# The running maximum of the cached pages, spread over the partitions by one rounded-type product of a high and a low part

## The chip, the cores and the metric

The kernel runs on one core of one Trainium2 chip. The metric is the device time of one execution in microseconds. The kernel must return the ten outputs of the reference; its inputs are float32.

## The reference

One inference step of one decoder layer. A prompt of 1024 tokens and eight sequences with eight new tokens each pass through an input projection; its columns feed a gated linear attention and a multi-head latent attention with eight heads. An output projection, a gated feed-forward part with a causal convolution, and a per-layer embedding follow.

The change concerns the latent attention of the eight sequences. Each has 64 cached pages of 128 positions, found by a page table. The softmax over the cached positions runs block by block, with a running maximum:

```python
def combine(a, b):
    m1, l1, acc1 = a
    m2, l2, acc2 = b
    m = jnp.maximum(m1, m2)
    c1 = jnp.exp(m1 - m)
    c2 = jnp.exp(m2 - m)
    return m, l1 * c1 + l2 * c2, acc1 * c1[..., None] + acc2 * c2[..., None]
...
def body(carry, phys):
    c = pool_ckv[phys]
    r = pool_krope[phys]
    k, v = latent_to_kv(c, r, w_kvup, g_kn)
    return combine(carry, block_stats(q, k, v, None)), None
```

In `block_stats`, m is the maximum of the block's scores, p the exponential of the scores less m, l their sum and acc the product of p with the values.

## The kernel before, in words

float32 products are made in most places by splitting both operands into a high part in the rounded type (`F32R`) and a low part, the remainder; `mm3` (lines 138 to 141) then sums three rounded products. `split` (line 114) makes the parts: a cast on ScalarE and a subtraction on VectorE or GpSimd.

The cached pages are worked through in 64 blocks, eight for each sequence; a block is eight pages and, in the first block of a sequence, the new tokens too. The generator `cache_stream` (line 678) runs its stages staggered over three blocks: `stage_load` fetches the pages by an indirect DMA; `pre` transposes the latents (`turn`, line 515) and makes the rope scores (`rope_scores`); `main` (line 543) makes the key products `ks`, squares them on ScalarE (line 560) and sums the squares on VectorE (line 565); `stage_b` (line 580) normalises the scores `sn`, a tile of 128 positions by pages by 64 pairs of head and token, and takes the maximum over the pages into `ml`, which holds the 64 columns twice (lines 598 and 599); `stage_c1` (line 606) handles the maximum; `stage_pv` multiplies by the latents.

In `stage_c1`, `ml` is transposed into PSUM (line 616), so that the 64 pairs lie on partitions, twice: 0 to 63 and 64 to 127. VectorE reduces over the positions and the earlier maximum `mo` into `m`, one column of 128 partitions (line 620 in the first block of a sequence, 622 in the others, there with an accumulator that is read by an instruction of its own). Line 625 spreads `m` over all partitions: the weights are the first 64 entries of `m`, repeated in 128 columns, and the moving operand is a 64x64 identity. The result, 128x64, is subtracted from the scores on VectorE (line 626); the exponential (628) and the split of the result (629, 630) follow. Line 635 works out the factor for the earlier sums from `m` and `mo`.

The blocks run beside the projections, the gated linear attention and the attention of the prompt (`dense`), which the loop at lines 1603 to 1614 interleaves with the blocks by a table of paces, and beside units of the output projection (`fill`) in the last blocks. The order on each engine's queue is set by the framework's planner, which simulates a timeline with its own costs of instructions. The feed-forward part comes behind all blocks.

`ones64`, four rows of 128 ones, is a source for a row of ones in the scratch tensor `dga`, written by three DMAs (lines 353 and, once for each half of the prompt, 857).

Of the kernel before, what the change touches and what calls it, by code (L numbers as in the profile page):

```python
# [8 lines left out]
F32 = mybir.dt.float32  # L9
F32R = mybir.dt.float32r  # L10
# [3 lines left out]
ALU = mybir.AluOpType  # L14
# [4 lines left out]
P = 128  # L19
D = 1024  # L20
T = 1024
# [3 lines left out]
R = NB * TS  # L25
# [19 lines left out]
def step_kernel(ctx: ExitStack, tc: tile.TileContext, A):  # L45
    nc = tc.nc
    pe, act, dve, pool, sp = nc.tensor, nc.scalar, nc.vector, nc.gpsimd, nc.sync
# [4 lines left out]
    def ctile(shape, dt, name):  # L52
        return const.tile(shape, dt, name=name, tag=name)
# [3 lines left out]
    ident = ctile([P, P], F32, "ident")  # L57
# [33 lines left out]
    dga = dram.tile([17, NTOK], F32, name="dga")  # L91
# [69 lines left out]
    def fold_rows(wk, ps, n, out, tag, bufs=None):  # L161
        t = wk.tile([R, 512], F32, tag=tag, name=tag, bufs=bufs)
        act.copy(t[:, :n], ps[R:2 * R, :n])
        dve.tensor_tensor(out, ps[0:R, :n], t[:, :n], ALU.add)
# [19 lines left out]
    cp = ph1.enter_context(tc.tile_pool(name="cp", bufs=1, side="right"))  # L184

    def pd(shape, name):
        return psD.tile(shape, F32, tag="d", name=name)
# [4 lines left out]
    def pm(shape, name):  # L192
        return psM.tile(shape, F32, tag="m", name=name)

    def cst(shape, dt, name):
        return cp.tile(shape, dt, name=name, tag=name)
# [4 lines left out]
    mv = [[cst([P, 576], F32R, f"mv{i}{s}") for s in "hl"] for i in range(2)]  # L201
    qbd = [[cst([P, 4, 64], F32R, f"qbd{i}{s}") for s in "hl"] for i in range(2)]
    chl = [cst([P, 9, 258], F32R, "chl")]
    ones64 = cst([4, P], F32, "ones64")
    pool.memset(ones64, 1.0)
    pool.memset(chl[0][:, :, 256:258].bitcast(F32), 1.0)
    newc = cst([P, 1, P], F32, "newc")
# [66 lines left out]
    def mm_lat(ps, x, w, first, last):  # L274

        if len(w.shape) == 3:
            ps = ps.rearrange("p (a c) -> p a c", a=2)
        pe.matmul(ps, x, w, start=first, stop=last)  # L278
# [64 lines left out]
    def sample_u(u, w):  # L343
        ps = pm([P, 512], "ps_sm")
        for k in range(8):
            for s in range(2):
                mm_lat(ps[:, :NL], xTs[:, k, :], w[s][k], k + s == 0, k + s == 8)
        fold_rows(wk, ps, NL, u[:R], "st", 3)
        pt = pm([P, 512], "pt_us")
        pe.transpose(pt[:16, :R], u[:R, 0:16], ident[:R, :R])  # L350
        act.copy(gaTs, pt[:16, :R])
        sp.dma_start(dga[1:17, T:], gaTs)
        sp.dma_start(dga[0:1, T:], ones64[0:1, 0:R])

    def sample_latents(u):
        cq = wk.tile([P, H, 96], F32, tag="qt", name="cq_s").rearrange("p h c -> p (h c)")[:, 0:256]
# [249 lines left out]
    def stage_c1(o):  # L606

        nt = o.nt
        sb = o.sn[:, :nt, :]
        mt = pm([P, 512], "mt")  # L610
        drain = o.n - NB * 8 + 3
        if drain == 1:
            fill(49 - z["units"])
        elif drain == 2:
            fill(2)
        pe.transpose(mt[:, 0:P], o.ml.rearrange("p a c -> p (a c)"), ident)
        m = cp.tile([P, 1], F32, tag="bm", name="bm", bufs=4)
        mo = state.get(o.b)
        if mo is None:
            dve.tensor_reduce(m, mt[:, 0:P], AX.X, ALU.max)  # L620
        else:
            dve.tensor_scalar(mt[:, 256:256 + P], mt[:, 0:P], mo, None, ALU.max, ALU.max, accum_out=m)
        if drain > 0:
            fill(1)
        pe.matmul(mt[:, P:P + 64], m[0:64].broadcast_to([64, P]), ident[0:64, 0:64], start=True, stop=True)
        dve.tensor_tensor(sb, sb, mt[:, P:P + 64].unsqueeze(1).broadcast_to([P, nt, 64]), ALU.subtract)
        phl = cp.tile([P, 9, P], F32R, tag="phl", name="phl", bufs=1)
        act.activation(sb, sb, AF.Exp)
        act.copy(phl[:, :nt, 0:64], sb)  # L629
        pool.tensor_tensor(phl[:, :nt, 64:128], sb, phl[:, :nt, 0:64].bitcast(F32), ALU.subtract)  # L630
        o.phl = phl
        o.t = None
        if mo is not None:
            o.t = cp.tile([P, 1], F32, tag="mb", name="mb", bufs=4)
            act.activation(o.t, m, AF.Exp, bias=mo, scale=-1.0)
        state[o.b] = m
# [41 lines left out]
    def cache_stream():  # L678
# [7 lines left out]
        for n in range(N + 2):  # L686
            z["block"] = n
            if n + 2 < N:
                blk[n + 2] = stage_load(*todo[n + 2], n + 2)
            if n < N:  # L690
                pre(blk, blk[n], 4)
                main(blk[n], 0)
            if 0 <= n - 2:
                stage_pv(blk[n - 2])
            if 0 <= n - 1 < N:
                stage_b(blk[n - 1])
            yield
            if n < N:
                if blk[n].nt == 9:
                    pre(blk, blk[n], 8)  # L700
                    main(blk[n], 4)
                    pre(blk, blk[n + 1], 0)
                    main(blk[n], 8)
                else:
                    if n + 1 < N:
                        pre(blk, blk[n + 1], 0)
                    main(blk[n], 4)
            if 0 <= n - 1 < N:
                stage_c1(blk[n - 1])
            if 0 <= n - 2:  # L710
                stage_c2(blk.pop(n - 2))
            yield
# [12 lines left out]
    def prompt_half(hf):  # L725
# [3 lines left out]
        hs = slice(hf * 512, hf * 512 + 512)  # L729
# [45 lines left out]
        if hf == 0:  # L775
            sample_x()
            load_x()
            wl = load_lat([chl[0][:, 2 * k:2 * k + 2, 0:NL // 2] for k in range(4)])
            load_x()
            load_constants()  # L780
            u = wk.tile([P, NL], F32, tag="u", name="u_s")
            sample_u(u, wl)
# [67 lines left out]
        def rank():  # L850
            pt = pd([P, 4, P], "pt_ga")
            for i in range(4):
                pe.transpose(pt[:16, i], lat[:, i, 0:16], ident)
            ga = wk.tile([P, 512], F32, tag="st", name="ga", bufs=3)
            act.copy(ga[:16], pt[:16].rearrange("p i c -> p (i c)"))
            sp.dma_start(dga[1:17, hs], ga[:16])
            sp.dma_start(dga[0, hs].rearrange("(a b) -> a b", a=4), ones64[0:4])

        def norm_latents(i):
            t = 4 * hf + i  # L860
# [87 lines left out]

        yield from mix(PLAN[0])
        rank()  # L950
        for i in range(4):
            norm_latents(i)
# [642 lines left out]
    def fill(n):  # L1595
        for _ in range(n):
            z["units"] += next(z["fill"], done) is None
# [302 lines left out]
    h, hs = z["h"], z["hs"]  # L1900
# [334 lines left out]
def build(arrays):  # L2235
    import concourse.bacc as _bacc

    nc = _bacc.Bacc("TRN2", target_bir_lowering=False, num_devices=1)
    A = {k: nc.dram_tensor(k, v.shape, mybir.dt.from_np(v.dtype), kind="ExternalInput").ap() for k, v in arrays.items()}
    for k, s in _OUTS:  # L2240
        A[k] = nc.dram_tensor(k, s, F32, kind="ExternalOutput").ap()
    with tile.TileContext(nc, schedule_with_timeline_sim=True) as tc:
        step_kernel(tc, A)
    return nc
# [11 lines left out]
```

## Time and profile before

| | us |
|---|---|
| median of 3 runs | 2219.15 (2218.44 to 2219.22) |
| profiled execution, device time | 2221.39 |
| its span, first to last instruction | 2219.6 |
| TensorE busy in the span | 2134.6 |
| VectorE busy in the span | 1666.6 |
| ScalarE busy in the span | 1369.1 |
| GpSimd busy in the span | 1227.5 |

The granted TensorE clock of the profiled execution was 0.984 of full speed. In profile lines PE is TensorE's products, PEld its weight loads, DVE VectorE, ACT ScalarE, POOL GpSimd, SP SyncE. A line in order of time has the start and the duration in us, engine, line of the kernel, operation, output tile and inputs, sizes and a count; in brackets stand the idle time before it and what ended that. A line of a group has the smallest, median and largest duration in ns and the starts of the first and the last. Products overlap in TensorE's pipeline, so the distance of their starts tells more than their durations.

### The profile page before, as it was taken

The page shows a single profiled execution, that of the slowest core. Times are in us where ns is not written, and L with a number is a line of the kernel's source. Part 1 is how long each engine was busy: PE and PEld are TensorE (multiplying, and loading weights), DVE is VectorE, ACT ScalarE, POOL GpSimd, SP SyncE. Part 2 cuts the span into 40 slices and gives each one's busy share as a digit, 9 for nine tenths or more (in the row PEclk, how much of TensorE's full clock was granted, in tenths as well). Part 3 has the DMA queues.
Part 4 walks back from the last instruction along what each step waited for, and adds up shares of the span by engine and source line. Part 5 has one row for each costly group of instructions (what it writes and reads, how often), then busy time and mean ns, then how long its engine had stood idle before and what let it go on. Part 6 is the DMA issues. An engine that isn't in the chain of part 4 may idle for free.

```text
span 2219.6 us, 38384 instructions
## 1 busy us (share of the span) xinstructions
PE 2134.6 (96%) x13460; PEld 1934.7 (87%) x13460; DVE 1666.6 (75%) x2551; ACT 1369.1 (62%) x3726; POOL 1227.5 (55%) x1330
## 2 busy tenths in 40 slices
PE   7999999999999999999999987999999999999999
PEld 6888978878888888887788876999999999888899
DVE  4775676467788888887888878888888886887642
ACT  5576766777778888887777766433333433534631
POOL 5675668576777777777445557666656562011100
PEclk9899999999999999999999998999999999999999
DMA  5343234412342222221521212322232325778321
GB/s 181 110 141 110 77 117 157 141 54 69 104 120 60 64 73 61 60 56 46 167 80 57 76 66 96 105 92 95 91 100 91 100 87 190 238 222 237 98 72 41
DMA packets 204418, 233.07 MB, mean 105 GB/s; under 512 B 42422, under 2 KB 146339, under 8 KB 204227
## 3 DMA queue, kind: packets, MB, share of 16 engines
q1 hardware_dynamic: 188259, 179.49, 25.8%
q0 software_dynamic: 14736, 46.67, 7.3%
q10 hardware_dynamic: 1232, 4.46, 0.5%
q8 instruction: 108, 1.77, 0.3%
q14 instruction: 83, 0.68, 0.1%
HBM read 188.00 MB, written 42.52 MB: 104 GB/s over the span
## 4 chain that ended last, share of the span: by engine, by line
PE 80%; DVE 7%; ACT 5%; DMA 4%; POOL 2%; issue 2%; SPq 0%; DVEq 0%; POOLq 0%; ACTq 0%
PE ps_gu L140 7%; PE ps_gu L141 7%; PE ps_gu L139 7%; PE ks L139 5%; PE ks L141 5%; PE ks L140 4%; PE ps_dn L141 3%; PE ps_dn L140 3%; PE ps_dn L139 3%; PE cpv L645 2%; PE ctp L522 2%; PE ps_lt L278 2%; PE ps_pj L139 2%; PE ps_pj L140 1%; PE ps_pj L141 1%
## 5 line engine op out<-in xcount | busy, mean ns | idle before, releaser
L560 ACT ACTIVATE csq<-ks 128x256 f32<-128x256 f32 x1040 | 392.2, 400 | 88.1 <-PE ks L141 78.0
L565 DVE TENSOR_REDUCE css<-csq 128x16 f32<-128x1024 f32 (+1 forms) x264 | 315.8, 1197 | 63.0 <-ACT csq L560 61.9
L115 ACT CAST wh<-st 128x512 fp32r<-128x512 f32 x176 | 108.4, 619 | 188.6 <-PE ps_gu L140 166.0
L139 PE MATMUL ks<-mv0h,cTh 128*128 128x320 f32 (+1 forms) x520 | 171.9, 333 | 6.9 <-ACT csq L560 3.0
L139 PE MATMUL ks<-mv1h,cTh 128*128 128x320 f32 (+1 forms) x520 | 170.4, 329 | 7.6 <-ACT sn L562 3.6
L604 POOL TENSOR_TENSOR chl<-craw,chl 128x1024 fp32r<-128x1024 f32 x64 | 141.8, 2216 | 57.9 <-ACT chl L603 57.2
L140 PE MATMUL ks<-mv1l,cTh 128*128 128x320 f32 (+1 forms) x520 | 154.0, 298 | 0.0
L140 PE MATMUL ks<-mv0l,cTh 128*128 128x320 f32 (+1 forms) x520 | 153.0, 296 | 0.0
L141 PE MATMUL ks<-mv0h,cTl 128*128 128x320 f32 (+1 forms) x520 | 148.6, 298 | 0.9 <-DVE cTl L116 0.8
L141 PE MATMUL ks<-mv1h,cTl 128*128 128x320 f32 (+1 forms) x520 | 148.9, 300 | 0.0
L630 POOL TENSOR_TENSOR phl<-sn,phl 128x512 fp32r<-128x512 f32 (+1 forms) x64 | 84.8, 1326 | 108.2 <-ACT phl L629 107.9
L116 DVE TENSOR_TENSOR wl<-st,wh 128x512 fp32r<-128x512 f32 x132 | 119.0, 903 | 28.5 <-ACT wh L115 28.5
L116 POOL TENSOR_TENSOR wl<-st,wh 128x512 fp32r<-128x512 f32 x44 | 69.4, 1580 | 103.5 <-ACT wh L115 98.2
L141 PE MATMUL ps_dn<-o 128*128 128x512 f32 x308 | 120.2, 390 | 0.0
L140 PE MATMUL ps_dn<-o 128*128 128x512 f32 x308 | 120.1, 390 | 0.1
L116 DVE TENSOR_TENSOR cTl<-ctp,cTh 128x512 fp32r<-128x512 f32 (+1 forms) x136 | 90.1, 663 | 39.4 <-ACT cTh L115 38.4
L139 PEld LDWEIGHTS ks<-mv0h,cTh 128*128 128x128 f32 x520 | 99.1, 191 | 20.7 <-ACT sn L562 7.1
L562 ACT COPY sn<-ks 128x64 f32<-128x64 f32 x520 | 116.8, 225 | 0.0
L139 PEld LDWEIGHTS ks<-mv1h,cTh 128*128 128x128 f32 x520 | 99.6, 191 | 19.7 <-ACT sn L562 7.4
L1317 POOL TENSOR_TENSOR pl<-p,ph 128x512 fp32r<-128x512 f32 (+1 forms) x96 | 97.1, 1016 | 31.7 <-DVE ph L1316 21.5
L139 PE MATMUL ps_dn<-o 128*128 128x512 f32 x308 | 112.1, 390 | 0.0
L139 PE MATMUL ps_gu<-xrh,wh 128*128 128x320 f32 x352 | 108.6, 309 | 1.1 <-ACT xrh L115 1.1
(672 smaller groups left out, 7875.3 us busy)
## 6 DMA issues: line engine op xcount, KB each, us to landing
raw<-ds SPq DMA_DIRECT2D x77, 256.0 KB
raw<-ffn_w_down SPq DMA_DIRECT2D x66, 256.0 KB
stage<-w_in SPq DMA_DIRECT2D x48, 256.0 KB
st<-ffn_w_gate SPq DMA_DIRECT2D x44, 256.0 KB
st<-ffn_w_up SPq DMA_DIRECT2D x44, 256.0 KB
wr<-ffn_w_down SPq DMA_DIRECT2D x44, 256.0 KB
ds<-cv SPq DMA_DIRECT2D x21, 512.0 KB
oraw<-doT SPq DMA_DIRECT2D x16, 256.0 KB
```

The source lines that it names most:

```text
L115: cast = act.copy(hi, src)
L116: res = (lo_eng or dve).tensor_tensor(lo, src, hi.bitcast(F32), ALU.subtract)
L139: pe.matmul(ps, ah, bh, start=first, stop=False)
L140: pe.matmul(ps, ah, bl, start=False, stop=False)
L141: return pe.matmul(ps, al, bh, start=False, stop=last)
L278: pe.matmul(ps, x, w, start=first, stop=last)
L560: act.activation(sq[:, f * 256:f * 256 + 256], ks[:, 0:256], AF.Square)
L562: act.copy(o.sn[:, g0 + i, :], ks[:, 256:320])
L565: dve.tensor_reduce(o.ss[:, g0 + i + 1 - n:g0 + i + 1, :].rearrange("p i h -> p (i h)"), sq2[:, :n].rearrange("p i (h n) -> p (i h) n", n= ...
L604: pool.tensor_tensor(ch[:, c0:c1, 128:256], src, ch[:, c0:c1, 0:128].bitcast(F32), ALU.subtract)
L630: pool.tensor_tensor(phl[:, :nt, 64:128], sb, phl[:, :nt, 0:64].bitcast(F32), ALU.subtract)
L1317: pool.tensor_tensor(pl[:, c0:], p[:, c0:], ph[:, c0:].bitcast(F32), ALU.subtract)
```

## The change

The maximum is copied to a tile `mr` in the rounded type; on partitions 64 to 127, which hold the same 64 values a second time, the copy is replaced by the remainder, `m` less the rounded value. One product over 128 partitions with two stacked 64x64 identities (`id2`, rounded type, made once at the start by two copies on ScalarE) adds high and low part and spreads the sum. `ones64` becomes 16 rows of 32 ones, and the DMAs that read it are written for that shape.

```diff
@@ -201,7 +201,10 @@
     chl = [cst([P, 9, 258], F32R, "chl")]
-    ones64 = cst([4, P], F32, "ones64")
+    id2 = cst([P, 64], F32R, "id2")
+    for s in range(2):
+        act.copy(id2[s * 64:s * 64 + 64], ident[s * 64:s * 64 + 64, s * 64:s * 64 + 64])
+    ones64 = cst([16, 32], F32, "ones64")
     pool.memset(ones64, 1.0)
@@ -350,7 +353,7 @@
         sp.dma_start(dga[1:17, T:], gaTs)
-        sp.dma_start(dga[0:1, T:], ones64[0:1, 0:R])
+        sp.dma_start(dga[0, T:].rearrange("(a b) -> a b", a=2), ones64[0:2])
@@ -622,7 +625,10 @@
         if drain > 0:
             fill(1)
-        pe.matmul(mt[:, P:P + 64], m[0:64].broadcast_to([64, P]), ident[0:64, 0:64], start=True, stop=True)
+        mr = cp.tile([P, 1], F32R, tag="mr", name="mr", bufs=2)
+        dve.tensor_copy(mr, m)
+        dve.tensor_tensor(mr[64:P], m[64:P], mr[64:P].bitcast(F32), ALU.subtract)
+        pe.matmul(mt[:, P:P + 64], mr.broadcast_to([P, P]), id2, start=True, stop=True)
         dve.tensor_tensor(sb, sb, mt[:, P:P + 64].unsqueeze(1).broadcast_to([P, nt, 64]), ALU.subtract)
@@ -854,7 +860,7 @@
             sp.dma_start(dga[1:17, hs], ga[:16])
-            sp.dma_start(dga[0, hs].rearrange("(a b) -> a b", a=4), ones64[0:4])
+            sp.dma_start(dga[0, hs].rearrange("(a b) -> a b", a=16), ones64)
```

## The prediction

> **What bounds the kernel now.** I began with the page: busy time by engine and the chain that ended last. Then the windows view, to see the stretch in which the edited line runs, and at last the order of time on TensorE and VectorE around it.
>
> ```profile
> span 2219.6 us, 38384 instructions
> PE 2134.6 (96%) x13460; PEld 1934.7 (87%) x13460; DVE 1666.6 (75%) x2551; ACT 1369.1 (62%) x3726; POOL 1227.5 (55%) x1330
> PE 80%; DVE 7%; ACT 5%; DMA 4%; POOL 2%; issue 2%; SPq 0%; DVEq 0%; POOLq 0%; ACTq 0%
> ```
> ```profile
> core 0: us, PE busy (x) PEld busy (x) DVE busy (x) ACT busy (x) POOL busy (x), PEclk, DMA share, GB/s
> 112.00:1330.00 1218.00, 1168.58 (x7763) 1029.74 (x7762) 923.92 (x1506) 935.10 (x2864) 803.46 (x870) 0.98 0.30 89
> 1330.00:2219.60 889.60, 871.93 (x5195) 821.89 (x5193) 675.39 (x897) 367.92 (x671) 357.06 (x348) 0.99 0.39 122
> ```
>
> TensorE paces the kernel: busy for 96% of the span, and 80% of the chain that ended last. The 64 cache blocks lie in the 1218 us from 112 to 1330, where TensorE is busy for 1168.58 us (96%), VectorE for 923.92 (76%), ScalarE for 935.10 (77%). The 890 us behind it are not touched by the change. So a removed TensorE microsecond in this stretch should mostly shorten the run, and an added VectorE microsecond should mostly not; the exceptions are the places where TensorE stands waiting for the very VectorE step that becomes longer.
>
> **The product that is replaced.** Two stretches of TensorE's order of time show what the product costs (line 625; the fp32 form runs as two passes, shown as x2). I read distances between starts, since the durations of pipelined products overlap.
>
> ```profile
> 1285.43 0.31 PE L141 MATMUL ks<-mv1h,cTl 128*128 128x320 f32 x1
> 1285.58 0.27 PE L616 MATMUL mt<-ident,ml 128*128 128x128 f32 x1
> 1285.61 0.36 PE L139 MATMUL ks<-mv1h,cTh 128*128 128x256 f32 x1
> 1285.81 0.28 PE L140 MATMUL ks<-mv1l,cTh 128*128 128x256 f32 x1
> 1285.93 0.29 PE L141 MATMUL ks<-mv1h,cTl 128*128 128x256 f32 x1
> 1286.05 0.31 PE L139 MATMUL ks<-mv1h,cTh 128*128 128x320 f32 x1
> 1286.20 0.31 PE L140 MATMUL ks<-mv1l,cTh 128*128 128x320 f32 x1
> 1286.34 0.31 PE L141 MATMUL ks<-mv1h,cTl 128*128 128x320 f32 x1
> 1286.58 0.43 PE L625 MATMUL mt<-ident,bm 64*128 64x64 f32 x2
> 1286.94 0.38 PE L139 MATMUL ks<-mv1h,cTh 128*128 128x256 f32 x1
> 1287.16 0.28 PE L140 MATMUL ks<-mv1l,cTh 128*128 128x256 f32 x1
> 1287.28 0.28 PE L141 MATMUL ks<-mv1h,cTl 128*128 128x256 f32 x1
> ...
> 639.22 0.28 PE L140 MATMUL ks<-mv1l,cTh 128*128 128x256 f32 x1
> 639.34 0.28 PE L141 MATMUL ks<-mv1h,cTl 128*128 128x256 f32 x1
> 639.55 0.43 PE L625 MATMUL mt<-ident,bm 64*128 64x64 f32 x2
> 639.91 0.66 PE L522 MATMUL ctp<-ident,craw 128*128 128x128 f32 x4
> ```
> ```profile
> L625 PEld LDWEIGHTS mt<-ident,bm x128: 182/185/245, 116.8 to 1325.9; 64*128 64x128 f32 x128
> L622 DVE DVE_READ_ACCUMULATOR mt<-mt,bm x56: 134/141/152, 151.8 to 1324.3; 128x1 f32 x56
> L620 DVE TENSOR_REDUCE bm<-mt x8: 270/277/773, 114.3 to 1223.6; 128x1 f32<-128x128 f32 x8
> ```
>
> In steady state a 320-wide product of lines 139 to 141 takes 0.145 us to the next start (1286.05 to 1286.20) and a 256-wide one 0.12 (1285.81 to 1285.93). Around line 625 three distances are long. The product in front takes 0.24 (1286.34 to 1286.58) instead of 0.145: 0.095 more. The two passes take 0.36 (1286.58 to 1286.94). The product behind takes 0.22 (1286.94 to 1287.16) instead of 0.12: 0.10 more. Sum 0.555 us. In the second stretch the next work is a fp32 transposition; 0.21 - 0.12 + 0.36 = 0.45 without anything behind it. Read in this way over all 64 blocks (first at 116.8, last at 1325.9), the mean is 0.53 us; I take that.
>
> **The product that comes.** Rounded type, 128 rows, 64 columns, one pass. No such form is in the trace; two rows stand near. The transposition of line 616 has 128 rows, waits for a small tile of another engine, and lies in the same stream: from 1285.58 to 1285.81 it and one 256-wide product take 0.23, so it costs 0.23 - 0.12 = 0.11 us. And the 64-wide rounded product of the rope scores has 0.13 us to the next start:
>
> ```profile
> 631.62 0.30 PE L139 MATMUL csr<-qbd1h,kTh 128*128 128x64 f32 x1
> 631.75 0.28 PE L140 MATMUL csr<-qbd1l,kTh 128*128 128x64 f32 x1
> ```
>
> I take 0.12. Saved per block 0.53 - 0.12 = 0.41 us, over 64 blocks 26.2 us. Upper bound 64 x (0.555 - 0.11) = 28.5. Lower bound: both gaps stay and only the two passes go, 64 x (0.36 - 0.13) = 14.7.
>
> Which bound holds hangs on what the gaps are. At 1286.58 the product was not waiting for its operand (the accumulator read below ends at 1286.31), so the gap in front is not a wait for VectorE. What sets line 625 apart from line 616, which has no gaps, are its 64 rows instead of 128 and its fp32 passes; the new product has neither. [...]
>
> Not all of it arrives. Where the chain runs through another engine, a shorter TensorE queue is only a longer wait. The chain's TensorE share (80%) and TensorE's busy share of the stretch (96%) bound the part that counts; I take 0.85, so 22.3 us.
>
> **What is added on VectorE.** Behind each maximum come a copy to the rounded type (128x1) and a subtraction (64x1), both ahead of the product. Nearest rows: a 128x1 cast, a 64x1 reciprocal, and two dependent small operations:
>
> ```profile
> L447 DVE CAST pf<-pidx x1: 153/153/153, 3.5 to 3.5; 128x1 f32<-128x1 int32 x1
> L669 DVE RECIPROCAL rl<-acclo x7: 142/145/155, 320.5 to 1224.4; 64x1 f32<-64x1 f32 x7
> ```
> ```profile
> 634.44 0.22 DVE L589 SCALAR_TENSOR_TENSOR ca<-css,ca 128x72 f32<-128x72 f32 x1
> 634.70 0.23 DVE L590 SCALAR_TENSOR_TENSOR cy<-ca,cy 128x72 f32<-128x72 f32 x1
> ...
> 1283.93 1.22 DVE L565 TENSOR_REDUCE css<-csq 128x16 f32<-128x1024 f32 x1 [0.24 <-ACT csq L560]
> ...
> 1285.89 0.36 DVE L622 TENSOR_SCALAR_CACHE_REDUCE mt<-mt,bm 128x128 f32<-128x128 f32 x1 [0.15 <-PE mt L616]
> 1286.17 0.14 DVE L622 DVE_READ_ACCUMULATOR mt<-mt,bm 128x1 f32 x1
> 1286.17 0.69 DVE L116 TENSOR_TENSOR cTl<-ctp,cTh 128x512 fp32r<-128x512 f32 x1
> ```
>
> Each is about 0.15 us, and a dependent step starts 0.04 after the end of the one before (634.66 to 634.70): 2 x 0.19 = 0.38 us later for the product's operand. The bounds are 0.15 (both nearly overlapped) and 0.38 plus one long reduction between them, the slow rival below. [...]
>
> Queued behind these two on VectorE are the remainders of the page latents (line 116), the square sums (line 565) and the scaling (589, 590), which others read; 64 x 0.38 = 24.3 us, against 1218 - 923.92 = 294 us in which VectorE is idle. By its chain share of 7% it costs 1.7 us.
>
> What the later operand costs TensorE is decided by the time between the end of the maximum and the product's weight load. Of the 64 pairs (their first and last starts are in the rows above) 8 have no slack: TensorE is already waiting. In four the slack is 0.02 to 0.3 us, and in 52 over 0.55. A delay of 0.38 thus costs 8 x 0.38 plus 0.7 for the four: 3.7 us. The waits view agrees that few blocks wait at all:
>
> ```profile
> PEld mt L625 <- DVE mt L622: 6.9, 7, 2.9
> DVE sn L626 <- PE mt L625: 11.9, 16, 1.8
> ```
>
> The subtraction of line 626 gets its operand later by 0.38 less what one pass saves against two (0.43 against the 0.27 of line 616): 0.22 us. It waits for TensorE now in 16 blocks, at most 3.5 us on an engine with room; nothing taken beyond the 1.7.
>
> **The rest.** Two copies of 64x64 on ScalarE at the start, hidden: ScalarE is idle for 2.54 us there until the first input lands. Were it not, two copies of a cast smaller than 0.36 us would cost under 0.7 us.
>
> ```profile
> 4.62 1.06 ACT L122 ACTIVATE junk<-xin_s 64x1024 bf16<-64x1024 f32 x1 [2.54 <-DMA xin_s<-x_sample]
> 9.48 0.36 ACT L115 CAST xTs<-pt 128x256 fp32r<-128x256 f32 x1
> ```
>
> The row of ones goes out in 16 pieces instead of 4 (and 2 instead of 1) from the same three SyncE issues, to be read much later; its memset becomes narrower. Nothing for these. SBUF use falls by a little.
>
> **Sum.** 22.3 saved, less 3.7, less 1.7: 16.9 us. The profiled execution took 2221.4 us (its span 2219.6 and 1.8 around it), so 2204.5; it lies 2.2 above the median of the runs, 2219.15, which gives 2202.
>
> **The rivals.** *Gaps stay.* The stalls before and behind the product belong to reading a one-column operand that was just written, not to 64 rows or fp32. Against it: line 616 reads a fresh tile without them. Then 14.7 x 0.85 = 12.5, less 5.4: 7 us faster, 2212.
>
> *No change.* TensorE's freed time is handed to ScalarE and VectorE, both busy for three quarters of the stretch, since the block's squares (line 560) and square sums must follow the products. For it: 50 us of TensorE idle exist already. Against it: these are 4% of the stretch. If under a quarter of the 26.2 arrives, it is eaten by the 5.4: 2219.
>
> *Slower.* The instruction order is made by a planner on modelled costs, and the two new steps may come apart in VectorE's queue. One square sum (line 565, 1.2 us) between them makes the operand 1.6 us late; 37 of the 64 products would then wait, by their present slack 34 us in all, against 22.3 - 1.7: 13 us slower, 2232. It decides from a delay of about 1.2 us in every block, where the waits reach 20.4 us. Against it: the two steps are ready back to back and short.
>
> **How the numbers follow.** Forecast 0.65, gaps stay 0.14, no change 0.09, slower 0.12. A measurement of this kernel can tell about 0.2%, 4.4 us, from no change. The forecast and the first rival lie beyond that on the fast side: faster 0.79, same 0.09, slower 0.12. The likeliest time is 2202. The low end has the upper bound of the saving arriving whole (28.5) with the waits small: 2190. The high end takes in the partial and the no-change case and leaves out the slow one: 2221.
>
> **What would show it.** In the changed profile line 625 (then 631) has 64 products and 64 weight loads of 128 rows instead of 128 of 64 rows, with 0.11 to 0.13 us of TensorE each and no long starts around them; two new VectorE groups of 64, about 0.15 us each; the weight loads' waits for VectorE near 10.6 us instead of 6.9; the stretch with the blocks ends near 1313 instead of 1330; and the part behind keeps its 890 us. I am wrong if the gaps stand around the new product, if the part behind 1330 changes, or if TensorE's idle time in the stretch grows by over 10 us.

## The result: 1.6% slower, not 0.8% faster

The changed kernel takes 2254.57 us in the median (2249.33 to 2258.98), the kernel before beside it 2219.15 us (2218.14 to 2223.53). The ratio is 1.0155, 95% interval 1.0143 to 1.0167: about 34 us lost, where 17 had been forecast as won. The profiled execution took 2251.68 us.

First the page of the changed kernel, the rows that answer to the first ones of before: span, busy time by engine, and the engines' shares of the chain that ended last.

```profile
span 2250.0 us, 38342 instructions
PE 2125.1 (94%) x13396; PEld 1928.4 (86%) x13396; DVE 1710.4 (76%) x2679; ACT 1370.9 (61%) x3728; POOL 1226.2 (54%) x1330
PE 69%; DVE 12%; ACT 7%; DMA 4%; POOL 4%; issue 4%; SPq 0%; DVEq 0%; POOLq 0%; ACTq 0%
```

Then the windows view, with its border where the blocks end now, at 1360 us:

```profile
core 0: us, PE busy (x) PEld busy (x) DVE busy (x) ACT busy (x) POOL busy (x), PEclk, DMA share, GB/s
112.00:1360.00 1248.00, 1162.07 (x7710) 1026.23 (x7709) 969.06 (x1637) 937.79 (x2866) 804.88 (x872) 0.98 0.29 87
1360.00:2250.00 890.00, 869.92 (x5186) 820.27 (x5185) 674.70 (x895) 366.98 (x669) 355.94 (x346) 0.99 0.39 122
```

The part behind the blocks keeps its 890 us. All the loss lies in the stretch with the blocks: 1248 us instead of 1218. TensorE is busy in it for 6.5 us less (1162.07 against 1168.58) and idle for 85.9 us instead of 49.4 (1218 - 1168.58). The chain tells the same: TensorE's share falls from 80% to 69%, VectorE's rises from 7% to 12%.

The product itself costs what was forecast. TensorE in order of time, at one of its places:

```profile
1286.28 0.28 PE L140 MATMUL ks<-mv1l,cTh 128*128 128x256 f32 x1
1286.40 0.28 PE L141 MATMUL ks<-mv1h,cTl 128*128 128x256 f32 x1
1286.52 0.19 PE L631 MATMUL mt<-id,mr 128*128 128x64 f32 x1
1286.55 0.39 PE L139 MATMUL ks<-mv1h,cTh 128*128 128x320 f32 x1
1286.78 0.31 PE L140 MATMUL ks<-mv1l,cTh 128*128 128x320 f32 x1
```

The product in front takes its usual 0.12 us to the next start, line 631 takes 0.03, the 320-wide product behind it 0.23 instead of 0.145. That is 0.03 + 0.085 = 0.115 us in all, where 0.12 had been taken. The odd rows are VectorE's. The groups of the tile `mr`, with the smallest, median and largest duration in ns, and below them who waited for it (us in total, times):

```profile
L629 DVE CAST mr<-bm x64: 130/153/155, 115.0 to 1351.6; 128x1 fp32r<-128x1 f32 x64
L630 DVE TENSOR_TENSOR mr<-bm,mr x64: 155/157/5345, 115.2 to 1351.8; 64x1 fp32r<-64x1 f32 x64
...
  PEld mt L631: 12.8, 11
  PE mt L631: 10.3, 11
  DVE sn L632: 9.3, 14
```

The median of the subtraction is 0.157 us as forecast, but its largest is 5.345 us. VectorE, GpSimd and TensorE in order of time around that one:

```profile
918.01 0.15 DVE L629 CAST mr<-bm 128x1 fp32r<-128x1 f32 x1
918.20 5.34 DVE L630 TENSOR_TENSOR mr<-bm,mr 64x1 fp32r<-64x1 f32 x1
923.58 0.69 DVE L1287 TENSOR_REDUCE amx<-t 128x1 f32<-128x512 f32 x1
```
```profile
917.79 0.95 POOL L476 DMA_INDIRECT craw<-cache_ckv,idx  x1 [0.30 <-issue]
918.76 1.30 POOL L1323 TENSOR_TENSOR pl<-p,ph 128x512 fp32r<-128x512 f32 x1
920.02 1.08 POOL L595 TENSOR_TENSOR sn<-sn,cy 128x512 f32<-128x512 f32 x1
921.05 1.26 POOL L116 TENSOR_TENSOR vo<-ldv,vo 128x512 fp32r<-128x512 f32 x1
922.27 1.25 POOL L597 TENSOR_TENSOR sn<-sn,sr 128x512 f32<-128x512 f32 x1
```
```profile
923.60 0.39 PE L631 MATMUL mt<-id,mr 128*128 128x64 f32 x1 [3.27 <-DVE mr L630]
```

The subtraction of 64 numbers lasts until GpSimd has finished its next four instructions, which follow back to back on an indirect DMA (922.27 + 1.25 = 923.52; the subtraction ends at 923.54), and TensorE stands idle for 3.27 us. It isn't alone: 24 of the 64 subtractions last over 0.4 us, 28.7 us together, and each of the 24 ends 14 to 30 ns behind the end of a GpSimd instruction.

This stall is followed by a second loss. Two windows of the same trace, the first from the last products before the stall to the one that waited, the second right behind it, and TensorE in order of time in the second:

```profile
920.27:923.69 3.42, 0.15 (x2) 0.09 (x1) 3.39 (x2) 1.50 (x6) 3.25 (x3) 1.00 0.30 116
923.69:927.10 3.41, 3.41 (x13) 2.96 (x14) 3.38 (x6) 0.65 (x3) 0.05 (x1) 0.50 0.00 0
```
```profile
926.06 0.41 PE L139 MATMUL ks<-mv1h,cTh 128*128 128x256 f32 x1
926.27 0.41 PE L140 MATMUL ks<-mv1l,cTh 128*128 128x256 f32 x1
926.48 0.41 PE L141 MATMUL ks<-mv1h,cTl 128*128 128x256 f32 x1
```

For the 3.41 us behind the stall the granted clock is 0.50, and a 256-wide product takes 0.21 us to the next start instead of 0.12. Between 112 and 1360 us this trace has 11 stretches at that clock, 51.2 us in all; before, there were 9 between 112 and 1330 us, 37.5 us in all. Over the whole span the granted clock is 0.981 instead of 0.984.

In 24 of the 64 blocks, mostly others than those with a long subtraction, the planner also put other work on VectorE between the copy and the subtraction, which then starts 0.18 to 1.56 us behind the copy's end instead of 0.03. Here it is a square sum (the accumulator read ends the maximum):

```profile
1066.42 0.13 DVE L625 DVE_READ_ACCUMULATOR mt<-mt,bm 128x1 f32 x1
1066.58 0.15 DVE L629 CAST mr<-bm 128x1 fp32r<-128x1 f32 x1
1067.04 1.22 DVE L568 TENSOR_REDUCE css<-csq 128x16 f32<-128x1024 f32 x1 [0.30 <-ACT csq L563]
1068.29 0.16 DVE L630 TENSOR_TENSOR mr<-bm,mr 64x1 fp32r<-64x1 f32 x1
```

Two theories follow. *Port*, as the expectations call it: a VectorE operation with two inputs in SBUF stands still while GpSimd works, as the subtraction at 918.20 us did (5.34 us instead of 0.157); by what means it is held up no run shows. *Order*: the planner laid other queues, and those are worse whatever the product does. How far the queues differ can be counted in the traces: without the added instructions and the product itself, another tile or another size stands at 5938 of 13332 places of TensorE's sequence, and at 1267 of 2551 of VectorE's. Outside the expectations, which count in another way, distances between orders are given in this count.

### The profile page after: what moved, and what is told of

Its sections match the earlier page's. It is cut to its first block, busy times and chain, and to the rows that moved or that the text cites. A ratio compares the mean times of both kernels' runs of the same rounds, so it can differ in the third digit from the quotient of the medians.

```text
span 2250.0 us, 38342 instructions
## 1 busy us (share of the span) xinstructions
PE 2125.1 (94%) x13396; PEld 1928.4 (86%) x13396; DVE 1710.4 (76%) x2679; ACT 1370.9 (61%) x3728; POOL 1226.2 (54%) x1330
## 4 chain that ended last, share of the span: by engine, by line
PE 69%; DVE 12%; ACT 7%; DMA 4%; POOL 4%; issue 4%; SPq 0%; DVEq 0%; POOLq 0%; ACTq 0%
PE ps_gu L141 7%; PE ps_gu L139 7%; PE ps_gu L140 7%; PE ks L139 4%; PE ks L141 4%; PE ks L140 3%; PE ps_dn L141 3%; PE ps_dn L140 3%; PE ps_dn L139 3%; DVE css L568 2%; PE cpv L651 2%; ACT csq L563 2%; PE ctp L525 1%; PE ps_pj L139 1%; PE ps_pj L140 1%
## 5 line engine op out<-in xcount | busy, mean ns | idle before, releaser
L141 PE MATMUL ps_gu<-xrh,wl 128*128 128x320 f32 x352 | 108.7, 309 | 0.0
```

The lines of the kernel that those rows point to most:

```text
L141: return pe.matmul(ps, al, bh, start=False, stop=last)
```

## Experiments

To part the two, a computation is held to another kernel's order: that kernel is planned first, and between every two neighbours on each engine's queue an edge of issue order is added, in outline as below; the added VectorE steps stand right behind their maximum in every block. In these kernels the product and its steps stand in a function of their own, at lines above 2200. Ratios are to the kernel before, with the 95% interval.

```diff
+for e, queue in planned_of_other_kernel:
+    for a, b in zip(queue, queue[1:]):
+        tc.add_manual_dep(of[b], of[a].name, info, reason="order")
```

**The change in the order of before, and the order of the change without the change.** The first keeps the new computation and the queues of before; the second keeps the fp32 product of before and the queues of the changed kernel.

> The changed computation, with every engine's instruction order held to that of the kernel before; the two new VectorE steps stand right behind the maximum. Theory order (the loss comes from the planner's new order): the gain of my prediction arrives, 2200 to 2208 us. Theory port (the remainder, a VectorE instruction with two SBUF inputs, stands still while a GpSimd instruction runs): some twenty of the 64 subtractions still last over 0.5 us, 25 us of VectorE in all, and the time is 2215 to 2235 us.

Measured: 2226.86 us, 1.0033 (1.0021 to 1.0046).

> The old plain product, without the two VectorE steps, with every engine's order held to that of the changed kernel. Theory order: slower than the changed kernel by what the product costs more, 2260 to 2275 us. Theory port: near the kernel before, 2215 to 2230 us, since only the long steps are gone.

Measured: 2243.4 us, 1.0109 (1.0093 to 1.0126). Neither theory carries the loss alone: in the order of before 0.3% of the 1.55% is left (19 of the 64 subtractions still last over 0.4 us, 20.4 us together), and the order alone loses 1.1% with the untouched computation.

**The remainder with one tensor input.** The rounded value becomes the scalar operand of the instruction:

```diff
-dve.tensor_tensor(mr[64:P], m[64:P], mr[64:P].bitcast(F32), ALU.subtract)
+dve.tensor_scalar(mr[64:P], m[64:P], mr[64:P].bitcast(F32), None, ALU.subtract)
```

> The changed computation in the changed kernel's own order, with the remainder as a tensor_scalar whose subtrahend is a scalar operand, so that it reads one tensor. Theory port: all 64 take about 0.15 us and the time falls by 20 to 35 us, to 2220 to 2235. Theory order: it stays within 8 us of the changed kernel, 2246 to 2256, the steps long or short.

Measured: 2232.64 us, 1.0062 (1.0046 to 1.0079).

> The changed computation in the order of the kernel before, with the remainder as a tensor_scalar that reads one tensor. Theory port: what the same edit took off in the new order (22 us) goes here too, 2227 to 2202..2210 us, and no step lasts over 0.3 us. Rival, the operand's lateness: two chained steps in front of the product cost by their 0.4 us whatever their form, and it stays at 2218 to 2227.

Measured: 2215.93 us, 0.9977 (0.9964 to 0.999). The group of this subtraction, held to the order of before:

```profile
L2336 DVE TENSOR_SCALAR mr<-bm,mr x64: 212/214/218, 115.5 to 1317.9; 64x1 fp32r<-64x1 f32 x64
```

and that of the two-input one in the same order:

```profile
L2332 DVE TENSOR_TENSOR mr<-bm,mr x64: 156/157/4426, 114.6 to 1327.7; 64x1 fp32r<-64x1 f32 x64
```

The one-input form is 57 ns longer in the median, yet none of its 64 exceeds 0.218 us. In the order of before, where both forms stand right behind the maximum and nothing else differs, it wins 1.0033 - 0.9977 = 0.56% (12.4 us). The port theory holds. In the order of the change the difference is 1.0155 - 1.0062 = 0.93% (20.6 us), but that isn't the form alone: the held kernel also has the two steps next to each other, where the changed kernel has them apart in 24 blocks. The scalar operand lies in SBUF too; why the instruction waits for GpSimd with a second tensor and not with that operand, no run shows.

**The product alone.** The maximum itself is written in the rounded type by the reduction, so no step is added; what is left out is the low part, that is, the blocks subtract a rounded maximum, the same one everywhere.

```diff
-m = cp.tile([P, 1], F32, tag="bm", name="bm", bufs=4)
+m = cp.tile([P, 1], F32R, tag="bm", name="bm", bufs=4)
-pe.matmul(mt[:, P:P + 64], m[0:64].broadcast_to([64, P]), ident[0:64, 0:64], start=True, stop=True)
+pe.matmul(mt[:, P:P + 64], m.broadcast_to([P, P]), id2, start=True, stop=True)
+act.copy(id2, ident[:, 0:64])   # lower 64 rows are zero
```

> The product alone: the maximum itself is kept in the rounded type, written so by the reduction, and used so everywhere; the softmax needs no exact maximum, only the same one in all places. No VectorE step is added; one rounded product over 128 rows, the lower half of its moving operand zero; the order is that of the kernel before. By my sum 26 us of TensorE saved, of which 0.85 arrive: 2196 to 2202. If the freed time turns into waits for other engines: 2206 to 2216.

Measured: 2208.93 us, 0.9954 (0.9936 to 0.9972): 10.2 us faster than before.

> The rounded maximum without added steps, the order left to the planner. Theory order (a newly laid order costs 10 to 25 us against the one of the kernel before, whatever is computed): 2208 to 2224 us. If the loss of order in the changed kernel came from its own two steps, which the planner prices wrongly: within 5 us of the same kernel in the old order.

Measured: 2234.49 us, 1.0068 (1.0042 to 1.0093). This is a third order, laid by the planner for a computation with no added step, and it loses 1.14% against the same computation in the order of before (25 us).

**128 rows, still fp32.** Only the count of rows changes, from 64 to 128, against the identity's first 64 columns, whose lower 64 rows are zero; the planner lays the same order as before by itself.

```diff
-pe.matmul(mt[:, P:P + 64], m[0:64].broadcast_to([64, P]), ident[0:64, 0:64], start=True, stop=True)
+pe.matmul(mt[:, P:P + 64], m.broadcast_to([P, P]), ident[:, 0:64], start=True, stop=True)
```

> The plain fp32 product, but over 128 rows: weights are all of m, the moving operand is the first 64 columns of the identity, whose lower half is zero. No step is added, and the planned order is that of the kernel before. If the stalls in front of and behind the product come from its 64 rows: they go, 0.1 to 0.2 us in each of 64 blocks, 6 to 12 us faster, 2207 to 2213. If they come from fp32: no change, 2217 to 2221.

Measured: 2210.01 us, 0.9959 (0.9947 to 0.997). Read by the distances between starts as in the prediction, medians over the 64 places: the excess in front of the product, the two passes, and the excess behind were 0.093, 0.361 and 0.104 us before; with 128 rows they are 0.001, 0.166 and 0.084; with the rounded type as well 0.002, 0.031 and 0.083. So 0.307 of the 0.558 us went with the 64 rows, though the type and the two passes stayed, and 0.135 with the type. Of the 0.307, 0.195 lay within the passes and 0.092 in front; the excess behind went by 0.02 only and stays in all forms. How the 64 rows cost this no run shows.

**The steps alone.** The fp32 product stays, and the copy and the two-input subtraction are made and read by nobody.

> The two VectorE steps alone, in the order of the kernel before: the copy and the remainder are made behind each maximum and read by nobody; the product is the old fp32 one and reads the maximum. Theory port: some twenty remainders still last over 0.5 us, and VectorE's queue behind them is late: 2228 to 2245 us. Rival, lateness of the operand: with nobody waiting for them they cost little, 2219 to 2225.

Measured: 2237.83 us, 1.0073 (1.0044 to 1.0102), 16.2 us slower. Here no product waits for the remainder, and the price is still as large, within the intervals, as in the whole change in the same order (1.0033 - 0.9954 = 0.79%). So it comes mainly through VectorE's queue: what stands behind the blocked subtraction is late, whether or not anyone wants its result.

**Small shifts of the order.** The numbers by which the blocks are paced beside the dense work are moved by 1%; nothing that is computed changes.

```diff
-PACE = [1.41, 1.088, 1.601, 1.168, 1.142, 0.708, 1.035, 1.027]
+PACE = [1.41, 1.098, 1.601, 1.168, 1.142, 0.708, 1.035, 1.027]   # old_pace_1098
+PACE = [1.41, 1.088, 1.601, 1.168, 1.142, 0.701, 1.035, 1.027]   # old_pace_0701, new_pace_0701
```

> The kernel before with one change that is no computation: the second number of the table of paces is 1.098 instead of 1.088, by which one stage of the cache blocks is taken up a little later beside the dense work, and the planner lays the queues anew (2277 of 13236 rows of TensorE stand elsewhere). Theory 'fitted order' (the order of before is an uncommonly good one, and any newly laid one loses): slower, by 5 to 20 us, ratio 1.002 to 1.009, less than the 23 us of the new orders so far because less of the order differs. Rival 'particular order' (the order laid for the new product has a fault of its own, such as GpSimd's late low parts of the exponentials): within 0.2% of before.

> The kernel before with the sixth number of the table of paces 0.701 instead of 0.708; no computation changes, and 2670 of 13236 rows of TensorE stand elsewhere. Theory 'fitted order': slower by 5 to 20 us, ratio 1.002 to 1.009. Rival 'particular order': within 0.2% of before.

> The changed kernel with the sixth number of the table of paces 0.701 instead of 0.708; its computation is that of the changed kernel, and 1383 rows of TensorE stand elsewhere than there. Theory 'fitted order': no order laid anew gets the loss back, ratio to before 1.010 to 1.020. Rival 'particular order': a shift can do away with the fault, ratio under 1.008.

Measured: 2224.64 us, 1.0030 (1.0019 to 1.0041); 2221.13 us, 1.0004 (0.9994 to 1.0014); and for the changed kernel 2232.54 us, 1.0058 (1.0041 to 1.0075). The first fits "fitted order", the second does not. The third says the most: its order is as far from that of before as the changed kernel's is (6403 of 13332 places against 5938), yet it costs only 1.0058 - 1.0033 = 0.25% over the same computation in the order of before. So an order laid anew need not lose 1%; the loss belongs to particular orders. In the last run TensorE's waits for GpSimd in the blocks fell from 16.7 to 7.9 us against the changed kernel; its longest subtraction is still 5.346 us.

> The changed kernel with the remainder as a one-input subtraction (the rounded value as the instruction's scalar operand), in the order that the planner lays for it, a third one (6777 rows of TensorE differ from the changed kernel's, 8048 from before's). Held to the order of before the same computation gave 0.9977, held to that of the changed kernel 1.0062. Theory 'fitted order': another 15 to 27 us over the order of before, ratio 1.004 to 1.010. Rival 'particular order': a different order has not the same fault, ratio 0.996 to 1.002.

Measured: 2235.76 us, 1.0075 (1.0055 to 1.0095). That is 0.98% over the same computation in the order of before. The four orders so far that lie far from that of before cost 1.22% (the changed kernel), 1.14, 0.98 and 0.25% over the same computation in the order of before; the two small shifts of that order cost 0 and 0.3%. This run also bears on the steps that come apart: its sequence on TensorE is near the changed kernel's (1140 places differ), it has other work between the steps in 22 blocks, and it is 0.13% slower than the same computation with the steps together in the changed kernel's order (1.0075 against 1.0062), less than the intervals can tell. So their coming apart seems to cost little, an estimated 9 us at most by the intervals if the 1140 places cost nothing; no run takes it alone.

**Which queue carries the order's loss.** The product alone again, with only some queues held to the order of before (all held: 0.9954; none: 1.0068).

```diff
 for e, queue in planned_of_other_kernel:
+    if e not in HELD:
+        continue
     for a, b in zip(queue, queue[1:]):
```

> The maximum kept in the rounded type, its product alone (no added steps); only TensorE's queue is held to the order of before, the other queues are laid by the planner around it (266 instructions of VectorE, 342 of ScalarE, 102 of GpSimd stand elsewhere than before). All queues held gave 0.9954, none 1.0068. Theory 'TensorE's sequence' (the loss lies in which products stand next to each other and when a block's come due): 0.994 to 0.998. Rival 'queues behind it' (VectorE, ScalarE and GpSimd work off their items in a worse sequence): 1.003 to 1.007.

> The same computation with every queue but TensorE's held to the order of before; 377 of 13236 rows of TensorE stand elsewhere. Theory 'TensorE's sequence': since the others tie it down to 377 rows, little can differ, 0.995 to 1.001, above the run with all held. Rival 'queues behind it': as with all held, 0.994 to 0.997. Over 1.003 would say that few displaced rows of TensorE cost it all.

> The same computation with GpSimd's queue alone held to the order of before; TensorE's order is laid anew (5188 rows elsewhere). Theory 'late low parts' (the loss comes from GpSimd reaching the low parts of the exponentials and of the prompt's attention late): at least half of it is regained, under 1.001. Theory 'TensorE's sequence': TensorE's order is again a new one, 1.003 to 1.009.

> The same computation with VectorE's queue alone held to the order of before (1129 rows of TensorE and 380 instructions of ScalarE elsewhere). Theory 'TensorE's sequence': between the two, 0.997 to 1.004, as about a sixth of the displaced rows is left. Rival 'queues behind it', with VectorE the one that matters: 0.994 to 0.998.

Measured: TensorE held 2229.56 us, 1.0050 (1.0033 to 1.0067); all but TensorE held 2211.71 us, 0.9964 (0.9952 to 0.9976); GpSimd held 2241.0 us, 1.0106 (1.0089 to 1.0123); VectorE held 2219.41 us, 1.0003 (0.9993 to 1.0012). With TensorE in its old sequence 0.96% of the 1.14% is lost all the same, so the theory "TensorE's sequence" falls. The second run says less: with the others held only 390 places of TensorE differ, so that TensorE's sequence had little room to do harm. GpSimd's own order as a cause falls too: held, it leaves the loss at 1.52%. Holding VectorE alone gets back about 0.65%, more than half, but it ties TensorE down as well (1300 places differ instead of 4643), and its 1.0003 lies above the 0.994 to 0.998 that was expected if VectorE's queue were the one that matters. The waits view of TensorE from 112 to 1330 us, with all queues held:

```profile
PE ks L139 <- ACT sn L562: 7.6, 16, 1.9
PE ks L139 <- ACT csq L560: 6.6, 13, 1.4
PE ks L139 <- ACT cTh L115: 4.8, 7, 1.3
```

and with TensorE alone held:

```profile
PE ks L139 <- ACT sn L562: 11.5, 21, 1.6
PE ks L139 <- ACT cTh L115: 6.2, 9, 1.4
PE ks L139 <- ACT csq L560: 5.6, 12, 1.4
PE pa L1177 <- POOL kx L1168: 3.8, 1, 3.8
```

The three waits of the key products for ScalarE grow from 19.0 to 23.3 us, and a single wait of 3.8 us for GpSimd comes, on a line that is not in the list of the other. That is a part of the 21 us (1.0050 - 0.9954 = 0.96%); which rows carry the rest stays open. Waits aren't all of it either. Between the rounded maximum with all queues held and with none, the same 13396 products keep TensorE busy for 2112.7 and 2121.6 us, with a granted clock of 0.986 and 0.981; so 8.9 of the 25.0 us between the two spans are products that take longer, and 16.1 are idle time. The stall at 920 us shows one place where the clock was low right behind idle time; whether the 8.9 us come from such places was not tested.

**The versions that beat both kernels** are among these runs: the rounded maximum in the order of before (0.9954) and the fp32 product over 128 rows (0.9959), whose intervals overlap. The second is the one line above and needs neither a step on VectorE nor an order held by hand.

## Why the prediction was wrong

The loss in its parts, each a difference of two ratios, times 2220 us:

| part | from | us | forecast |
|---|---|---|---|
| product alone | rounded maximum, order of before: 0.9954 | -10.2 | -22.3 |
| two steps, without blocking | one-input remainder, order of before, less that: 0.9977 - 0.9954 | +5.1 | +5.4 |
| VectorE's subtraction shut out by GpSimd | 1.0033 - 0.9977 | +12.4 | none |
| order laid anew, the two steps apart in 24 blocks with it | 1.0155 - 1.0033 | +27.1 | none (but for a rival's one case) |
| sum | 1.0155 | +34.4 | -16.9 |

The first intervals are some 4 us wide on either side, so the 5.1 is not known better than to about 5 us. The last two terms are not independent. With the one-input form and the steps together, the order costs 18.9 us (1.0062 - 0.9977); the 20.6 us that are then left hold more blocking than in the order of before (28.7 us in long subtractions against 20.4) and the steps' coming apart, and no run parts these.

*The step that failed most: the order.* The prediction took the queues as they are and asked what each would gain or lose. But a planner lays them from modelled durations, and with another product and two more steps it laid all of them anew. The slow rival named the planner, with one mishap: a square sum between the two steps, 1.6 us late in every block. "The two steps are ready back to back and short" was the argument against it, and that failed: in 24 of the 64 blocks they came apart, in six of these by a square sum, 0.84 us on average. So the rival saw a true mishap, but in three blocks of eight, and by the runs it isn't what cost most of the time: orders in which nothing can come apart (the rounded maximum, or the fp32 product held to the changed kernel's order) lose nearly as much.

*The step on VectorE's price.* "Each is about 0.15 us" was read from a cast and a reciprocal, operations of one input. The added subtraction has two, both in SBUF. Rows of two inputs stood in the profile of before, two of them in the prediction's own lines (589 and 590, 0.22 and 0.23 us), from which only the time between the end of the first and the start of the second was taken. Their groups, that of a 128x16 operation (line 101), and that of line 626, which has two inputs too but one of them, `mt`, in PSUM; below them the places on VectorE and on GpSimd where the longest of line 101 lies:

```profile
L589 DVE SCALAR_TENSOR_TENSOR ca<-css,ca x64: 206/225/2358, 104.7 to 1314.7; 128x64 f32<-128x64 f32 x56, 128x72 f32<-128x72 f32 x8
L590 DVE SCALAR_TENSOR_TENSOR cy<-ca,cy x64: 206/225/1325, 105.8 to 1315.0; 128x64 f32<-128x64 f32 x56, 128x72 f32<-128x72 f32 x8
L101 DVE SCALAR_TENSOR_TENSOR nwt<-nwt,qss x9: 160/176/2112, 55.3 to 360.5; 128x16 f32<-128x16 f32 x8, 64x16 f32<-64x16 f32 x1
L626 DVE TENSOR_TENSOR sn<-sn,mt x64: 665/681/755, 117.3 to 1327.2; 128x512 f32<-128x512 f32 x56, 128x576 f32<-128x576 f32 x8
```
```profile
126.19 2.11 DVE L101 SCALAR_TENSOR_TENSOR nwt<-nwt,qss 128x16 f32<-128x16 f32 x1
```
```profile
126.06 2.20 POOL L604 TENSOR_TENSOR chl<-craw,chl 128x1024 fp32r<-128x1024 f32 x1 [3.04 <-ACT chl L603]
```

In each block line 589 runs once, as the subtraction would: 0.225 us in the median, 2.358 at most, and 15 of the 64 over 0.4 us, 16.2 us together. The longest of line 101 ends 0.04 us behind GpSimd's. With GpSimd busy for 66% of the stretch (803.46 of 1218 us), such a step meets one often; line 626, with an input in PSUM, never takes over 0.755 us, though a GpSimd instruction runs beside 37 of its 64. The largest durations of lines 589, 590 and 101 would have warned of this. The durations without blocking were right, 0.153 and 0.157 us in the median, and +5.1 us for both steps without blocking agrees with the 5.4, though it is known to about 5 us only. The division of that into 3.7 for the operand and 1.7 for VectorE can't be tested so; the steps that nobody reads cost as much, within what the runs can tell, as those that are read.

*The saving.* The sum of the distances was right: the product costs 0.115 us where 0.12 stood, and the rival "gaps stay", with only the passes going, falls. Of the two gaps, though, only the one in front went; the one behind stays at 0.083 of 0.104 us. The prediction said that line 616 has no gaps, but its own rows show one behind it (0.20 instead of 0.12 us, 1285.61 to 1285.81), and its price of 0.11 us already held that gap. So the size came out right while the reason for the gap behind did not. What failed is the share that arrives, which was set at 0.85 and is nearer 0.43, with the interval of the 10.2 us some 0.3 to 0.6: by the distances, read as in the prediction, 0.37 us per block went in the mean (0.53 to 0.16), 23.4 us in all, and 10.2 came off. With 128 fp32 rows 17 us went and 9.1 came off. The rows of TensorE's waits from 112 to 1330 us in the profile of before show one taker:

```profile
PE ks L139 <- ACT sn L562: 6.3, 14, 1.6
PE ks L139 <- ACT csq L560: 4.2, 6, 1.4
PE ks L139 <- ACT cTh L115: 3.1, 6, 1.3
```

With the product alone, in the same order, these three became 7.6, 6.6 and 4.8 us (above): 5.4 us more waiting for ScalarE. On the page of that kernel:

```profile
span 2205.7 us, 38257 instructions
PE 2112.7 (96%) x13396; PEld 1921.4 (87%) x13396; DVE 1666.0 (76%) x2551; ACT 1366.0 (62%) x3727; POOL 1230.2 (56%) x1330
```

TensorE is busy for 21.9 us less than before, and idle for 8.0 us more (93.0 against 85.0); the two profiled spans differ by 13.9 us, the medians by the 10.2. This is the rival "no change" in part. A busy share of 96% says how much of the stretch TensorE works, not how much of a saved microsecond arrives: that is decided where the other engines come just in time. In the changed kernel, with the same product, TensorE's busy time fell by 9.5 us only (2134.6 to 2125.1); the other 12.4 us are lost on products that took longer, at a granted clock of 0.981 against 0.986.

*What was named as a sign of being wrong* came: TensorE's idle time in the stretch grew by 36.5 us, far over 10. The sign "weight loads wait near 10.6 us" was close for the wrong reason (12.8 us, a good part of it behind blocked subtractions and steps that had come apart; 3.5 us of it at the one of 5.345 us), and the stretch ended at 1360 instead of 1313 us. The part behind kept its 890 us. TensorE's first product on `mt` starts 0.4 us later (114.3 instead of 113.9), so the copies at the start cost no more than that there; the row of ones was not taken by itself.

## What to carry to other kernels

Where a planner lays the queues, a change of one instruction is two changes, the instruction and the order; hold the new computation to the old order before judging it; the order alone cost 0.25 to 1.2% here, and which it is can't be seen from how many places differ. Price a small VectorE step by rows with the same number of SBUF inputs and by their largest duration, not the median (2.358 and 0.225 us for line 589), wherever GpSimd is busy beside it, and try the form with one tensor input if there is one (0.218 us at most here, where the other took up to 4.426). Read the granted clock beside the idle time: a stall of TensorE can be paid twice (here 3.27 us idle, then 3.41 us at a clock of 0.50). Look for the cheapest half of a change: 128 rows instead of 64 brought nearly all that the rounded type did, without a step added.

## What the runs showed of the hardware

- A two-input VectorE operation of 0.157 us was shut out by several GpSimd instructions in a row, not only by the one that ran, in 6 of the 24 long subtractions of the changed kernel; in the other 18 one GpSimd instruction was already running when the subtraction started. The longest is 5.345 us through four of them, though it began 0.56 us ahead of the first of the four (918.20 to 918.76), beside the last 0.54 us of an indirect DMA on GpSimd; spans on GpSimd are rough. In four others of the six a GpSimd instruction was running when the subtraction started, and a next one, which started up to 0.80 us behind the subtraction, came ahead of it too.
- The one-input subtraction with a scalar operand has 0.214 us in the median and a spread of 6 ns (0.212 to 0.218), with GpSimd as busy beside it (1224.8 us in the span, against 1229.6 with the two-input form in the same order). Not every operation with one input is so even: the 16 casts `ph<-p` of 128x384 on VectorE (line 1316 of the kernel before) had 0.361 us in the median and 2.627 at most.
- A fp32 product over 64 rows among products over 128 cost 0.558 us by the distances of the starts, over 128 rows 0.251, and in the rounded type 0.116.
- Behind a stall of TensorE of 3.27 us the granted clock was 0.50 for 3.41 us, and the 256-wide products took 0.21 us from start to start instead of 0.12.
